# Position rows of the first expert table on ScalarE, and the adds of token pairs one pair later

## The chip, the cores and the metric

The kernel runs on one core of one Trainium2 chip. The metric is the device time of one launch in microseconds (us), lower is better; times of a kernel are given as the median of several runs. A profiled execution gives, beside its time, a trace of every instruction on the engines: TensorE (PE, with its weight loads as PEld), VectorE (DVE), ScalarE (ACT), GpSimd (POOL), and the DMA queues.

## What is computed

The reference is two transformer-like blocks over 256 tokens of width 1024, in float32. The change is in the last step of the second block, a retrieval of single-neuron experts:

```python
ts, ti = lax.top_k(s, K)                       # 16 best of 128 keys, twice per head, 8 heads
cs, ci = lax.top_k(cand.reshape(B, L, PEER_HEADS, K * K), K)
e1 = jnp.take_along_axis(ti[..., 0, :], ci // K, axis=-1)
e2 = jnp.take_along_axis(ti[..., 1, :], ci % K, axis=-1)
experts = e1 * N_KEYS + e2                     # 128 of 16384 experts per token
g = jax.nn.softmax(cs, axis=-1)
act = gelu(einsum('td,tkd->tk', xt, u_tab[experts])) * g
out = einsum('tk,tkd->td', act, v_tab[experts])
```

The kernel doesn't gather. It multiplies all tokens with the whole first table `u_tab` (16384 x 1024), takes the Gelu, multiplies by a dense table of weights that is zero for experts which a token didn't choose, and multiplies the result with the whole second table.

## The kernel before

**Units.** The weights come as blocks of 128x1024, 512 KB each, in one stream. `Stream.next` hands out a block as two parts whose sum is the float32 value: ScalarE casts the high part `wh` (line 244), VectorE subtracts it from the raw block to give the low part `wl` (line 251). It prepares them ahead: when unit n is asked for, the cast and the subtraction of unit n+3 are written into the queues of the two engines. There are three raw buffers, four of `wh`, four of `wl`. A unit of the first expert table is one product of 24 matmuls of 256 columns (`gemm_w`, lines 310 to 312). Two units fill one PSUM tile (`mm`, two buffers); behind the second one ScalarE takes the Gelu of both (line 1433) and its queue issues the store of the result to DRAM (line 1435).

**The dense weights.** The stage of the first expert table has 88 units; in the bursts behind the first 84 of them `weights_dense` builds `gd`, 128 x 128 x 256: first index by second index by token. For token t the rows of `eT` hold the 128 chosen first indices, second indices and weights. `o1` holds for each choice the row of zeros with a one at its first index (called position rows here), made for four tokens at once by a comparison with `iota` (line 1558; `ONE` is 4, two buffers). `oh` is the same for the second index, times the weight, in a high and a low half (line 1563; six buffers). Four steps later (`LAG`) a matmul of the two gives the token's 128x128 weights, halves side by side (line 1573). Two tokens share a PSUM tile (`acc`, three buffers). When the second of a pair is done, ScalarE copies the low halves into `gd` (line 1578) and VectorE adds the high halves (line 1579). The tile comes free when both have read it.

**Order.** Each engine works through its own queue in the order in which the program is written; a wait at the head of a queue holds all behind it. `paced` (line 1587) spreads the 260 steps of `weights_dense` (256 tokens and the lag) over 84 bursts, one behind each unit: three steps, in eight of the bursts four. So PE does 24 matmuls of a unit, three or four of L1573, then the next unit; ScalarE does the Gelu (behind every second unit), the copies of the burst, the cast for the next request; VectorE does the subtraction, then `o1`, `oh` and the add of each step.

Behind the stage comes the second expert table, which reads `gd`.

Of the kernel before, what the change touches and what calls it, by code (L numbers as in the profile page):

```python
# [10 lines left out]
F32 = mybir.dt.float32  # L11
# [4 lines left out]
AF = mybir.ActivationFunctionType  # L16
ALU = mybir.AluOpType
# [12 lines left out]
ONE = 4  # L30
# [237 lines left out]
class Pump:  # L268
# [3 lines left out]
    def add(self, gen, last=False):  # L272

        (self.last if last else self.active).append(gen)
# [15 lines left out]
def body(ctx, tc, a, o, upto=99):  # L290
    nc = tc.nc
# [6 lines left out]
    def psum(tag):  # L298
        return PS.tile([128, 512], F32, tag=tag, name=tag, bufs={"mm": 2, "acc": 3, "od": 1, "tr": 2}[tag])

    def accs():
        return [psum("acc"), psum("acc"), psum("acc"), psum("od")]
# [37 lines left out]
    def gemm_rows(acc, w, xh, xl, start, stop):  # L340
        h, lo = w
        for tt in range(2):
            ts_ = slice(tt * 128, tt * 128 + 128)
            for hf in range(2):
                cs = slice(hf * 512, hf * 512 + 512)
                mm3(acc[2 * tt + hf], xh[:, ts_], xl[:, ts_], h[:, cs], lo[:, cs], start, stop)

    def split(h, lo, src, eng=None):
        nc.scalar.copy(h, src)  # L349
        (eng or nc.vector).tensor_tensor(lo, src, h.bitcast(F32), op=ALU.subtract)  # L350
# [34 lines left out]
    def gain(i, pool):  # L385
        g = pool.tile([128, D], F32, tag="gain", name="gain", bufs=1)
        nc.gpsimd.dma_start(g, a["gains"][i:i + 1, :].to_broadcast([128, D]))
        return g
# [291 lines left out]
    with tc.tile_pool(name="mix", bufs=1) as MP:  # L680
# [285 lines left out]
        for c in range(8):  # L966
# [4 lines left out]
            t = sg[0][:, c, :]  # L971
# [25 lines left out]
        g = gain(POSTM, MP)  # L997
# [88 lines left out]
    with tc.tile_pool(name="b2", bufs=1) as BP:  # L1086
# [291 lines left out]
        for i in range(4):  # L1378
# [5 lines left out]
            t = th[:, 2 * i:2 * i + 2, :]  # L1384
# [37 lines left out]
    iota = PP.tile([128, 128], F32, name="iota")  # L1422
    eT = [PP.tile([128, 3, 128], F32, name=f"eT{tt}") for tt in range(2)]
    stored = [DP.tile([128, 8 if i < 15 else 4, T], F32, name=f"act{i}") for i in range(16)]

    def experts_in(i, between=pump.step):
        pt = psum("mm")
        gemm_w(pt[:, :T], ws.next(), xs_x)
        between()
        gemm_w(pt[:, T:], ws.next(), xs_x)  # L1430
        st = PP.tile([128, 2, T], F32, tag="st", name="st", bufs=2)
        last[i] = st
        nc.scalar.activation(st, pt.rearrange("p (e t) -> p e t", e=2), AF.Gelu_apprx_tanh)  # L1433
        if i < 62:
            nc.scalar.dma_start(stored[i // 4][:, 2 * (i % 4):2 * (i % 4) + 2, :], st)
# [3 lines left out]
    with tc.tile_pool(name="route", bufs=1) as RP:  # L1439
# [3 lines left out]
        v = RP.tile([128, 2, 16, 16], F32, name="v")  # L1443
# [99 lines left out]
    with tc.tile_pool(name="dense", bufs=1) as GP:  # L1543
        gd = GP.tile([128, 128, T], F32, name="gd")

        wp = GP.tile([128, 2, 128], F32R, name="wp")

        def weights_dense():

            o1s, ohs = {}, {}  # L1550
            for t in range(T + LAG):
                if t < T:
                    tt, tl = divmod(t, 128)
                    if tl == 0:
                        split(wp[:, 0], wp[:, 1], eT[tt][:, 2])
                    if t % ONE == 0:
                        o1 = GP.tile([128, ONE, 128], F32R, tag="oh1", name="oh1", bufs=2)
                        nc.vector.tensor_tensor(o1, iota[:, None, :].to_broadcast([128, ONE, 128]),  # L1558
                                                eT[tt][:, 0, tl:tl + ONE, None].to_broadcast([128, ONE, 128]),
                                                op=ALU.is_equal)  # L1560
                        o1s[t // ONE] = o1
                    oh = GP.tile([128, 2, 128], F32R, tag="ow", name="oh2", bufs=6)
                    nc.vector.scalar_tensor_tensor(oh, iota[:, None, :].to_broadcast([128, 2, 128]),  # L1563
                                                   eT[tt][:, 1, tl:tl + 1],
                                                   wp[:, :, tl:tl + 1].bitcast(F32).to_broadcast([128, 2, 128]),
                                                   op0=ALU.is_equal, op1=ALU.mult)
                    ohs[t] = oh
                u = t - LAG
                if u >= 0:
                    if u % 2 == 0:  # L1570
                        pt = psum("acc")
                    oh = ohs.pop(u)
                    nc.tensor.matmul(pt[:, u % 2 * T:u % 2 * T + T], o1s[u // ONE][:, u % ONE],  # L1573
                                     oh.rearrange("p n e -> p (n e)"), start=True, stop=True)
                    if u % 2 == 1:
                        v = pt.rearrange("p (t n e) -> p n e t", t=2, n=2)
                        g = gd[:, :, u - 1:u + 1]
                        nc.scalar.copy(g, v[:, 1])  # L1578
                        nc.vector.tensor_tensor(g, v[:, 0], g, op=ALU.add)  # L1579
                yield  # L1580

        pump.add(weights_dense())
        left = 128 - 2 * n_in[0]
        total = T + LAG
        busy = left - 4

        def paced(i):
            for _ in range(min(i + 1, busy) * total // busy - min(i, busy) * total // busy):
                pump.step()

        sv = {}

        def fetch(b):
            if b < 16:
                sv[b] = P0.tile([128, 8, T], F32, tag="lT" if b % 2 else "hT", name="sv")
                nc.gpsimd.dma_start(sv[b][:, :8 if b < 15 else 4, :], stored[b])

        order = list(range(124, 128)) + list(range(124))

        def act_split(n):  # L1600
            e = order[n]
            src = last[e // 2] if e >= 124 else sv[e // 8][:, e % 8 - e % 2:e % 8 - e % 2 + 2, :]
            if e % 2 == 0:
                nc.vector.tensor_tensor(src, src, gd[:, e:e + 2, :], op=ALU.mult)  # L1604
            ah = GP.tile([128, T], F32R, tag="ow", name="ah", bufs=6)
            al = GP.tile([128, T], F32R, tag="ow", name="al", bufs=6)
            split(ah, al, src[:, e % 2])
            if e % 8 == 7 and e < 120:
                fetch(e // 8 + 2)
            return ah, al  # L1610

        for i in range(left // 2):
            experts_in(n_in[0] + i, lambda: paced(2 * i))
            paced(2 * i + 1)
            if i == left // 2 - 2:
                pump.drain()
                ws.pool_every = 0
                nxt = [act_split(0), act_split(1)]
        fetch(0)
        fetch(1)  # L1620
        acc = accs()
        for n in range(126):
            nxt.append(act_split(n + 2))
            ah, al = nxt.pop(0)
            gemm_rows(acc, ws.next(), ah, al, n == 0, False)
        gf = P0.tile([128, D], F32, tag="raw", name="gf", bufs=RAW)
        nc.scalar.dma_start(gf, a["gains"][FINAL:FINAL + 1, :].to_broadcast([128, D]))
        x2 = [P0.tile([128, D], F32, tag="raw", name="x2", bufs=RAW) for tt in range(2)]
        for tt in range(2):
            nc.scalar.dma_start(x2[tt], res[tt * 128:(tt + 1) * 128, :])  # L1630
        finish(acc, [(ws.next(), *nxt[n]) for n in range(2)])
        jk = P0.tile([128, 1024], F32, tag="wh", name="jk", bufs=NH)
        ys = [P0.tile([128, D], F32, tag="wl", name="ys", bufs=NL) for tt in range(2)]
        rs = [None, None]

        def scaled(tt, hf):
            y = ys[tt][:, HALVES[hf]]
            if hf:
                nc.scalar.activation(y, y, AF.Copy, scale=rs[tt])
            else:  # L1640
                nc.vector.tensor_scalar(y, y, rs[tt], None, op0=ALU.mult)
            (nc.scalar if tt and hf else nc.sync).dma_start(o[tt * 128:tt * 128 + 128, HALVES[hf]], y)

        for tt in range(2):
            fn = RowNorm(GP, lambda hf: x2[tt][:, HALVES[hf]], jk[:, :512], 1.0)
            for hf, sl in enumerate(HALVES):
                nc.vector.tensor_tensor(x2[tt][:, sl], acc[2 * tt + hf], x2[tt][:, sl], op=ALU.add)
                fn.part(hf)
            if tt:
                scaled(0, 0)  # L1650
                scaled(0, 1)
            for sl in HALVES:
                nc.vector.tensor_tensor(ys[tt][:, sl], x2[tt][:, sl], gf[:, sl], op=ALU.mult)
            rs[tt] = fn.root()
        for hf in range(2):
            scaled(1, hf)
# [19 lines left out]
```

## Time and profile before

| | us |
|---|---|
| median of 3 runs | 1751.85 (1751.81 to 1753.88) |
| the profiled execution | 1750.99 |
| its span, first to last instruction | 1749.1 |
| busy PE / PEld | 1716.1 / 1571.1 |
| busy DVE / ACT / POOL | 1305.2 / 928.7 / 141.8 |
| the stage of the change, from 1104 to 1383 | 279 |

Busy time is the time in which at least one instruction of the engine was recorded. Matmuls are pipelined and their records overlap, so a PE that is busy all the time need not run at its peak; the distance between the starts of two matmuls tells that better. Records of the other engines overlap a little too, so what an instruction costs in a full queue is the distance from its start to the next one's.

### The profile page before, as it was taken

The page shows a single profiled execution, that of the slowest core. Times are in us where ns is not written, and L with a number is a line of the kernel's source. Part 1 is how long each engine was busy: PE and PEld are TensorE (multiplying, and loading weights), DVE is VectorE, ACT ScalarE, POOL GpSimd, SP SyncE. Part 2 cuts the span into 40 slices and gives each one's busy share as a digit, 9 for nine tenths or more (in the row PEclk, how much of TensorE's full clock was granted, in tenths as well). Part 3 has the DMA queues.
Part 4 walks back from the last instruction along what each step waited for, and adds up shares of the span by engine and source line. Part 5 has one row for each costly group of instructions (what it writes and reads, how often), then busy time and mean ns, then how long its engine had stood idle before and what let it go on. Part 6 is the DMA issues. An engine that isn't in the chain of part 4 may idle for free.

```text
span 1749.1 us, 30357 instructions
## 1 busy us (share of the span) xinstructions
PE 1716.1 (98%) x11768; PEld 1571.1 (90%) x11770; DVE 1305.2 (75%) x2238; ACT 928.7 (53%) x1518; POOL 141.8 (8%) x138
## 2 busy tenths in 40 slices
PE   8999999999999999999999999999999999999998
PEld 8999899999899987997899999999999988888886
DVE  5665677846765654878777999899999866667775
ACT  5544556654564445687345455555555545555444
POOL 2000000000100211000005624000000000000000
PEclk9999999999999999999899999999999999999999
DMA  7656454444476653563265576666665677777674
GB/s 246 189 172 198 149 181 147 141 148 138 137 227 190 195 166 119 169 194 109 74 193 196 184 226 216 221 193 199 194 199 188 215 250 250 238 252 240 241 243 166
DMA packets 93409, 332.05 MB, mean 190 GB/s; under 512 B 10553, under 2 KB 10708, under 8 KB 90961
## 3 DMA queue, kind: packets, MB, share of 16 engines
q1 hardware_dynamic: 79488, 287.73, 51.4%
q0 software_dynamic: 3696, 21.67, 3.5%
q10 hardware_dynamic: 10080, 20.71, 3.2%
q8 instruction: 92, 1.51, 0.4%
q14 instruction: 53, 0.43, 0.1%
HBM read 311.73 MB, written 18.35 MB: 189 GB/s over the span
## 4 chain that ended last, share of the span: by engine, by line
PE 78%; DVE 16%; issue 3%; ACT 1%; DMA 1%; POOL 0%; POOLq 0%; ACTq 0%; DVEq 0%
PE mm L310 13%; PE mm L312 13%; PE mm L311 13%; PE acc L312 8%; PE acc L310 8%; PE acc L311 8%; DVE oh L1563 5%; DVE wl L251 4%; PE od L310 2%; PE od L311 2%; PE od L312 2%; DVE gd L1579 2%; DVE oh L1558 2%; PE tr L1317 1%; PE acc L731 1%
## 5 line engine op out<-in xcount | busy, mean ns | idle before, releaser
L251 DVE TENSOR_TENSOR wl<-raw,wh 128x1024 fp32r<-128x1024 f32 x509 | 621.7, 1225 | 281.6 <-ACT wh L244 280.0
L310 PE MATMUL mm<-hT,wh 128*128 128x256 f32 (+1 forms) x2496 | 711.2, 285 | 0.4 <-ACT qb L1474 0.4
L311 PE MATMUL mm<-lT,wh 128*128 128x256 f32 (+1 forms) x2496 | 703.1, 282 | 0.0
L312 PE MATMUL mm<-hT,wl 128*128 128x256 f32 (+1 forms) x2496 | 702.7, 282 | 0.0
L244 ACT CAST wh<-raw 128x1024 fp32r<-128x1024 f32 x544 | 569.0, 1050 | 189.5 <-PE mm L311 71.4
L310 PEld LDWEIGHTS mm<-hT,wh 128*128 128x128 f32 x2496 | 471.7, 189 | 8.3 <-issue 3.9
L311 PEld LDWEIGHTS mm<-lT,wh 128*128 128x128 f32 x2496 | 470.5, 188 | 3.4 <-issue 1.4
L312 PEld LDWEIGHTS mm<-hT,wl 128*128 128x128 f32 x2496 | 472.1, 189 | 0.1
L310 PE MATMUL acc<-wh,ah 128*128 128x512 f32 x516 | 201.8, 391 | 0.0
L312 PE MATMUL acc<-wh,al 128*128 128x512 f32 x516 | 201.8, 391 | 0.0
L311 PE MATMUL acc<-wl,ah 128*128 128x512 f32 x516 | 201.6, 391 | 0.0
L349 ACT CAST ah<-sv 128x256 fp32r<-128x256 f32 x124 | 50.3, 406 | 152.6 <-DVE sv L1604 120.6
L312 PEld LDWEIGHTS acc<-wh,al 128*128 128x128 f32 x516 | 96.8, 188 | 20.8
L1563 DVE SCALAR_TENSOR_TENSOR oh<-iota,eT,wp 128x256 fp32r<-128x256 f32 x256 | 115.4, 479 | 0.0
L311 PEld LDWEIGHTS acc<-wl,ah 128*128 128x128 f32 x516 | 96.9, 188 | 19.6 <-issue 0.2
L310 PEld LDWEIGHTS acc<-wh,ah 128*128 128x128 f32 x516 | 97.0, 188 | 19.2 <-issue 0.3
L251 POOL TENSOR_TENSOR wl<-raw,wh 128x1024 fp32r<-128x1024 f32 x35 | 83.7, 2401 | 60.5 <-ACT wh L244 59.4
L1433 ACT ACTIVATE st<-mm 128x512 f32<-128x512 f32 x64 | 38.3, 599 | 94.3 <-PE mm L312 94.2
L350 DVE TENSOR_TENSOR al<-sv,ah 128x256 fp32r<-128x256 f32 x124 | 52.5, 424 | 35.0 <-ACT ah L349 35.0
L1578 ACT COPY gd<-acc 128x256 f32<-128x256 f32 x128 | 46.6, 402 | 59.3 <-PE acc L1573 43.4
L310 PE MATMUL od<-wh,ah 128*128 128x512 f32 x172 | 67.3, 391 | 0.0
L312 PE MATMUL od<-wh,al 128*128 128x512 f32 x172 | 67.2, 391 | 0.0
(400 smaller groups left out, 2041.9 us busy)
## 6 DMA issues: line engine op xcount, KB each, us to landing
raw<-in_ws_dram SPq DMA_DIRECT2D x288, 512.0 KB, 3.7
raw<-in_us_dram SPq DMA_DIRECT2D x128, 512.0 KB, 3.7
raw<-in_vs_dram SPq DMA_DIRECT2D x128, 512.0 KB, 4.2
act<-st ACTq DMA_DIRECT2D x62, 256.0 KB, 2.8
sv<-act POOLq DMA_DIRECT2D x15, 1024.0 KB, 7.1
gate_w<-in_gate_w_dram ACTq DMA_DIRECT2D x2, 1024.0 KB, 5.9
gain<-in_gains_dram POOLq DMA_DIRECT2D x3, 512.0 KB, 6.6
res<-x SPq DMA_DIRECT2D x2, 512.0 KB, 4.0
```

Of the source, the lines that this page charges most:

```text
L244: self.nc.scalar.copy(h, self.raw[i])
L251: eng.tensor_tensor(lo, self.raw.pop(i), h.bitcast(F32), op=ALU.subtract)
L310: nc.tensor.matmul(out, lh, rh, start=start, stop=False)
L311: nc.tensor.matmul(out, lh, rl, start=False, stop=False)
L312: nc.tensor.matmul(out, ll, rh, start=False, stop=stop)
L349: nc.scalar.copy(h, src)
L350: (eng or nc.vector).tensor_tensor(lo, src, h.bitcast(F32), op=ALU.subtract)
L1433: nc.scalar.activation(st, pt.rearrange("p (e t) -> p e t", e=2), AF.Gelu_apprx_tanh)
L1558: nc.vector.tensor_tensor(o1, iota[:, None, :].to_broadcast([128, ONE, 128]), eT[tt][:, 0, tl:tl + ONE, None].to_broadcast([128, ONE, 128] ...
L1563: nc.vector.scalar_tensor_tensor(oh, iota[:, None, :].to_broadcast([128, 2, 128]), eT[tt][:, 1, tl:tl + 1], wp[:, :, tl:tl + 1].bitcast(F3 ...
L1578: nc.scalar.copy(g, v[:, 1])
L1579: nc.vector.tensor_tensor(g, v[:, 0], g, op=ALU.add)
```

## The change

In `weights_dense` every second group of four tokens has its position rows made on ScalarE: four activations Abs(e - iota), one for each token, with the index as an operand per partition, and one Relu(1 - that) over all four, in place. The other groups stay on VectorE. The add of a token pair isn't written behind the copy of the same pair any more but behind the copy of the next pair; the last one comes after the loop.

```diff
-            o1s, ohs = {}, {}
+            o1s, ohs, copied = {}, {}, []
+
+            def add():
+                g, v = copied.pop(0)
+                nc.vector.tensor_tensor(g, v, g, op=ALU.add)
...
                         o1 = GP.tile([128, ONE, 128], F32R, tag="oh1", name="oh1", bufs=2)
-                        nc.vector.tensor_tensor(o1, iota[:, None, :].to_broadcast([128, ONE, 128]),
-                                                eT[tt][:, 0, tl:tl + ONE, None].to_broadcast([128, ONE, 128]),
-                                                op=ALU.is_equal)
+                        if t // ONE % 2:
+                            for j in range(ONE):
+                                nc.scalar.activation(o1[:, j], iota, AF.Abs, scale=-1.0,
+                                                     bias=eT[tt][:, 0, tl + j:tl + j + 1])
+                            nc.scalar.activation(o1, o1.bitcast(F32), AF.Relu, scale=-1.0, bias=1.0)
+                        else:
+                            nc.vector.tensor_tensor(o1, iota[:, None, :].to_broadcast([128, ONE, 128]),
+                                                    eT[tt][:, 0, tl:tl + ONE, None].to_broadcast([128, ONE, 128]),
+                                                    op=ALU.is_equal)
...
                         nc.scalar.copy(g, v[:, 1])
-                        nc.vector.tensor_tensor(g, v[:, 0], g, op=ALU.add)
-                yield
+                        copied.append((g, v[:, 0]))
+                        if len(copied) > 1:
+                            add()
+                yield
+            add()
```

## Rows read from the trace of the kernel before

**Rows 1.** Busy time by stage: length, then each engine's busy us and instructions.

```profile
core 0: us, PE busy (x) PEld busy (x) DVE busy (x) ACT busy (x) POOL busy (x), PEclk, DMA share, GB/s
1104.00:1383.00 279.00, 273.51 (x2254) 268.44 (x2254) 278.99 (x534) 148.56 (x255) 0.00 (x0) 1.00 0.62 198
```

**Rows 2.** Groups by line, VectorE, same stage: count, busy us, mean ns, idle before.

```profile
L1563 DVE SCALAR_TENSOR_TENSOR oh<-iota,eT,wp 128x256 fp32r<-128x256 f32 x256 | 115.4, 479 | 0.0
L251 DVE TENSOR_TENSOR wl<-raw,wh 128x1024 fp32r<-128x1024 f32 x84 | 102.2, 1217 | 0.8 <-ACT wh L244 0.8
L1579 DVE TENSOR_TENSOR gd<-acc,gd 128x256 f32<-128x256 f32 x128 | 55.8, 437 | 0.0
L1558 DVE TENSOR_TENSOR oh<-iota,eT 128x512 fp32r<-128x512 f32 x64 | 43.7, 683 | 0.0
```

**Rows 3.** Waits, same stage: who waited for whom, total us, times, longest.

```profile
PE acc L1573 <- DVE oh L1563: 3.6, 14, 0.5
...
DVE wl L251 <- ACT wh L244: 0.8, 1, 0.8
```

**Rows 4.** The matmuls of line 1573: duration in ns, first and last start.

```profile
L1573 PE MATMUL acc<-oh,oh x256: 279/282/385, 1105.8 to 1381.2; 128*128 128x256 f32 x128
```

**Rows 5.** Timeline of PE, line 1573 alone: start, length, engine, line, merged count.

```profile
1244.08 0.36 PE L1573 MATMUL acc<-oh,oh 128*128 128x256 f32 x1 [0.52 <-DVE oh L1563]
1247.08 0.52 PE L1573 MATMUL acc<-oh,oh 128*128 128x256 f32 x3
1250.29 0.52 PE L1573 MATMUL acc<-oh,oh 128*128 128x256 f32 x3
1253.49 0.52 PE L1573 MATMUL acc<-oh,oh 128*128 128x256 f32 x3
```

**Rows 6.** Timeline of VectorE in the middle of the stage.

```profile
1243.45 0.88 DVE L1563 SCALAR_TENSOR_TENSOR oh<-iota,eT,wp 128x256 fp32r<-128x256 f32 x2
...
1246.51 0.43 DVE L1579 TENSOR_TENSOR gd<-acc,gd 128x256 f32<-128x256 f32 x1
1246.86 0.68 DVE L1558 TENSOR_TENSOR oh<-iota,eT 128x512 fp32r<-128x512 f32 x1
1247.46 0.48 DVE L1563 SCALAR_TENSOR_TENSOR oh<-iota,eT,wp 128x256 fp32r<-128x256 f32 x1
1247.85 1.22 DVE L251 TENSOR_TENSOR wl<-raw,wh 128x1024 fp32r<-128x1024 f32 x1
1248.99 0.48 DVE L1563 SCALAR_TENSOR_TENSOR oh<-iota,eT,wp 128x256 fp32r<-128x256 f32 x1
```

**Rows 7.** Timeline of ScalarE over the same two bursts.

```profile
1247.28 0.60 ACT L1433 ACTIVATE st<-mm 128x512 f32<-128x512 f32 x1 [2.22 <-PE mm L312]
1247.91 0.33 ACTq L1435 DMA_DIRECT2D act<-st  x1
1248.28 0.69 ACT L1578 COPY gd<-acc 128x256 f32<-128x256 f32 x2 [0.40 <-ACT st L1433]
1248.83 1.06 ACT L244 CAST wh<-raw 128x1024 fp32r<-128x1024 f32 x1
1250.72 0.40 ACT L1578 COPY gd<-acc 128x256 f32<-128x256 f32 x1 [0.83 <-PE acc L1573]
1251.01 1.05 ACT L244 CAST wh<-raw 128x1024 fp32r<-128x1024 f32 x1
```

**Rows 8.** Timeline of ScalarE in earlier stages: activations with an operand per partition.

```profile
265.93 0.63 ACT L785 ACTIVATE ov<-tr,ls 128x128 f32<-128x128 f32 x2
...
762.04 0.52 ACT L1154 ACTIVATE aa<-rr,ncd 128x272 f32<-128x272 f32 x1
762.59 0.52 ACT L1155 ACTIVATE rr<-rr,cdec 128x272 f32<-128x272 f32 x1
763.02 0.41 ACT L1156 ACTIVATE ii<-aa 128x272 f32<-128x272 f32 x1
```

**Rows 9.** Table loads of the Gelu's line, and a square near the end.

```profile
L1433 ACT ACT_TABLE_LOAD  x2: 1283/1283/1283, 1022.3 to 1074.9; - x2
...
1739.24 0.64 ACT L424 ACTIVATE jk<-x 128x512 f32<-128x512 f32 x1 [6.02 <-DVE x L1647]
```

## The prediction

> **What bounds the kernel now.** I read the busy time by stage first. In the stage of the change, 1104 to 1383 us, VectorE (DVE) is busy 278.99 of 279.00 us, ScalarE (ACT) 148.56 and PE 273.51, at a granted clock of 1.00 (2.4 GHz) [rows 1]. So two engines look full, and the groups by line say with what: DVE makes 84 `wl`, 256 `oh`, 64 groups of position rows and 128 adds [rows 2]. The waits then tell DVE and PE apart: DVE waits once, for 0.8 us, while PE waits for DVE's `oh` 14 times [rows 3]. PE's own speed stands between undisturbed bursts: 1247.08, 1250.29 and 1253.49 are 54 matmuls in 6.41 us, 0.1187 us each [rows 5]. From the first L1573 matmul to the last, 1105.8 to 1381.2, lie 255 of them and 82 x 24 of the units, 2223 x 0.1187 = 263.9 of 275.4 us [rows 4]. So **PE loses about 11.5 us** here. That is the most that any relief of DVE can give in this stage.
>
> From start to start a DVE `wl` takes 1.14 us, an `oh` 0.39, a position group 0.60, an add 0.35 [rows 6]; 84 x 1.14 + 256 x 0.39 + 64 x 0.60 + 128 x 0.35 = 278.8. DVE is the bound, by its sum.
>
> **Part 1: every second position group goes to ScalarE.** Removed: 32 x 0.60 = 19.2 us of DVE, which leaves 259.6, less than PE's 263.9. Added: 32 times four Abs of 128x128 and one Relu of 128x512. No Abs or Relu is in the trace. The nearest row of the Abs' size, with an operand per partition as the Abs' bias is one, is L785: two in 0.63 us, so 0.26 from start to start and 0.37 whole [rows 8]. The Relu works in place on what the Abs wrote. L1155 overwrites what L1154 still reads and starts 0.55 after it, 0.03 behind its end; L1156, free of L1155, starts 0.43 after it, 0.09 before its end [rows 8]. So the fourth Abs counts 0.37 + 0.03 = 0.40, and the Relu, by a 128x512 ScalarE row of 0.64 [rows 9], counts 0.54, or 0.65 if its bias of 1.0 is an operand (the 0.11 between L1154 and L1156). The group is 3 x 0.26 + 0.40 + 0.54 to 0.65, I take **1.8 us**; from below four at 0.26 and a Relu at 0.54, 1.6; from above 4 x 0.40 + 0.72 = 2.3. All 32: 58 us, ScalarE 148.6 + 58 = 207 of 279. By its sum it isn't the bound. The Abs adds no wait: its buffer was last read by the matmul that the copy ahead of it in the queue has just waited for.
>
> What counts is what is queued behind. ScalarE works in order, and behind each burst stands the `wh` cast of the unit four ahead; DVE's `wl` waits for that cast, and all DVE work of the next burst stands behind that `wl`. Take E as the start of a burst's first matmul. Behind the second unit of a pair (E = 1247.08) the Gelu starts at E + 0.20, its store's issue holds the queue, the copies start at E + 1.20, the cast at E + 1.75, and it ends at E + 2.81; behind a first unit (E = 1250.29) the copy starts at E + 0.43 and the cast ends at E + 1.77 [rows 5, 7]. The position group goes in ahead of the cast in both.
>
> **Part 2: the add behind the next pair's copy.** No instruction is added but one call at the end. The add no longer waits for the copy just issued. Its price is elsewhere: the PSUM buffer of a pair (`acc`, three of them) comes free with its add. Before, the add stood five steps ahead of the matmul that takes the buffer again; now three. A burst is three steps (84 bursts, 260 steps: eight have four). So PE's burst j+2 needs adds that DVE makes in its section j+1, right behind the `wl` that waits for the cast of burst j.
>
> **The two together.** Let C be the cast's end, counted from E of burst j. PE starts burst j+2 at E + 6.40. It follows DVE by 0.15 (an `oh` from 1243.45, one of two in 0.88, ends 1243.93; its matmul starts 1244.08) [rows 5, 6]. DVE needs 0.03 and the `wl` (1.14), then its steps up to the add that PE wants, three steps ahead of a pair's first matmul, the last add whole (0.43). That matmul is the third of burst j+2 (at 6.64) if the burst begins with a pair, else the second (6.52). 1.20 is where ScalarE is free behind the Gelu, 0.28 a copy's share of two in 0.69, 1.05 the cast [rows 7]. t is the first step of a group on ScalarE:
> - t first in a gelu burst: C = 1.20 + 1.80 + 0.28 + 1.05 = 4.33. DVE then does `oh`, add, an even position group, `oh`, `oh`, add: 2.55. Ready at 4.33 + 1.17 + 2.55 = 8.05; PE wants it at 6.64 - 0.15 = 6.49. **1.56 late.**
> - t second: one copy more, C = 4.61; `oh`, `oh`, add, 1.21: 6.99 against 6.37, 0.62 late.
> - t third: C = 4.33; `oh`, add, `oh`, `oh`, add, 1.95: 7.45 against 6.49, 0.96 late.
> - in the other bursts, t first (its Abs start behind the cast of the burst before): C = 2.63, in time; second: C = 3.72, in time; third: C = 3.56, 0.19 late.
>
> A group comes each eight steps, bursts are three, their kinds alternate and the four-step ones shift the phase, so all six places are equally frequent: 3.33 us for six, 32 / 6 x 3.33 = **17.8 us**. Eight four-step sections are 1.14 + 4 x 0.39 + 2 x 0.35 + 0.30 = 3.70 of DVE against PE's 28 x 0.1187 = 3.32; with no slack left there, 8 x 0.38 = 3.0 more. Sum 20.8 us of stalls where there are 11.5: **+9.3 us**. Nothing behind the stage changes; it starts that much later. The profiled execution (span 1749.1, 1750.99 with what lies around it) would become 1760.3; on the median of 1751.85, **1761.2**. With the group at 1.6 the late terms are 1.36, 0.42, 0.76 and 0: 13.5 + 3.0 - 11.5 = +5; if the four-step sections find slack too, +2. At 2.3 they are 2.06, 1.12, 1.46 and 0.69, and the two places in time become late by 0.36 and 0.23: 31.6 + 3.0 - 11.5 = +23. Own range: 1754 to 1775.
>
> The Trainium skill (Perfetto Trace Analysis, section Optimizing Scalar/DVE Operations) says that with DVE saturated, giving some of its work to ScalarE may make sense; on busy sums alone that speaks for a gain, and it is the first rival. Its section Optimization Strategy says that a gap which keeps coming back on the engine that should be full can mean too few PSUM buffers; by the steps above that would be the sight of the changed stage.
>
> **Rivals.**
> 1. *Faster: PE becomes the bound.* If DVE's relief counts and the casts come in time, PE runs at 0.1187 per matmul and the 11.5 us go: 1740. For it: 207 of 279 us on ScalarE, and DVE 4 us below PE. Against it: DVE would have to wait almost nowhere, since its slack is 0.05 us per burst, and C = 4.3 to 4.6 in half of the places. Two of those three come in time only if a group costs ScalarE under about 0.8 us. Half the loss given back would be 1746.
> 2. *No difference.* The late casts meet a DVE that is still behind from before, so that part of the lateness isn't waited for; stalls then change owner, from `oh` to adds, at about the old 11.5 us: 1750 to 1755.
> 3. *The change doesn't do what it says: table loads.* If Abs or Relu were outside of the Gelu's table, each group would cost two loads of 1.28 us [rows 9], 32 x 2.57 = 82 us on ScalarE: 289 us and its 40 pauses of 0.4 behind the Gelu's store issue, 305 us for a stage of 279: 1778 at least. Against it: the squares at 1739 run with no load since the one for the Gelu at 1074.9 [rows 9]. The Trainium skill (ScalarE: Activation LUTs, section Table sets) states that relu and abs are in every set; no row of before has either.
>
> **How the numbers follow.** Forecast 0.70, rival 1 0.14, rival 2 0.13, rival 3 0.03. What a measurement of this kernel tells from no change is about 0.2%, 3.5 us. Faster by more than that is rival 1, 0.14; within it most of rival 2 and the forecast's low edge, 0.15; slower 0.71. The range takes the forecast's own and reaches down into rival 2; rival 1, rival 3 and the last of the high end are left out: 1750 to 1772.
>
> **What would show it.** Right: in the new stage DVE idles 20 us or more, nearly all in front of L251 on the `wh` cast; PE's waits at L1573 grow to some 21 us and name the add rather than `oh`, in stalls of 0.6 to 1.6 us a burst or two behind a ScalarE group in a gelu burst; the ScalarE group takes 1.7 to 1.9 us; the stage is 286 to 291 us long. Wrong: a stage of 268 us with DVE idle in many short waits (rival 1); or PE's waits unchanged (rival 2); or ACT_TABLE_LOAD in the stage (rival 3). The weakest step is that DVE stands waiting when a late cast comes: if it is still busy with earlier work at C, the lateness counts less.

## The result and the profile after

The changed kernel takes 1768.43 us (median of 4 runs, 1764.48 to 1770.54), the kernel before 1751.83 beside it: ratio 1.010, 95% interval 1.0085 to 1.0116. It is slower by 16.6 us, inside the range of 1750 to 1772; the forecast was 9.3 us of loss. The span of the profiled execution went from 1749.1 to 1766.2. No median or ratio here or below has in it three single executions of e1, e2 and e8 that took 3436 to 7906 us.

The stage by busy time (length, then each engine's busy us and instructions, granted clock, DMA), then the matmuls of line 1573 before, now line 1586 (duration in ns, first and last start), then what PE's two sequences, the weight loads and the matmuls, waited for in front of them:

```profile
1104.00:1400.00 296.00, 277.70 (x2258) 271.55 (x2257) 262.55 (x501) 203.15 (x415) 0.00 (x0) 0.99 0.60 186
```

```profile
L1586 PE MATMUL acc<-oh,oh x256: 277/282/387, 1106.1 to 1398.3; 128*128 128x256 f32 x128
```

```profile
  DVE gd L1556: 29.3, 43
  ACT wh L244: 5.9, 3
```

The same list for line 1573 before:

```profile
  issue: 6.7, 19
  DVE oh L1563: 3.6, 14
  ACT gd L1578: 1.6, 3
  ACT st L1433: 1.5, 3
  ACT wh L244: 0.7, 1
```

The new stage is 17 us longer than the old one in [rows 1], and first to last matmul of the token pairs take 292.2 us where they took 275.4 [rows 4]: the whole loss is here, +16.8. At 0.1187 us per matmul 263.9 of it is PE's own, so PE loses 28.3 us where it lost 11.5. VectorE (DVE), which was busy for 278.99 of 279.00 us [rows 1], is idle for 33.4 of 296. And PE now waits for the add, `gd` of line 1556; before, no wait for the add is in the list. These lists add up both sequences of PE, and most stalls stand in both, once for the weight load and once for the matmul, sometimes under two names: the 5.9 us for the cast are three weight loads whose matmuls wait for the add. So 29.3 isn't a time lost; 28.3 is, and it has everything in it.

The groups of the stage by line (count, busy us, mean ns, idle before and for whom):

```profile
L251 DVE TENSOR_TENSOR wl<-raw,wh 128x1024 fp32r<-128x1024 f32 x84 | 102.3, 1217 | 31.4 <-ACT wh L244 31.4
L1567 ACT ACTIVATE oh<-iota,eT 128x128 fp32r<-128x128 f32 x128 | 40.9, 395 | 2.4 <-ACT st L1433 2.4
L1569 ACT ACTIVATE oh<-oh 128x512 fp32r<-128x512 f32 x32 | 20.3, 633 | 1.0
```

DVE's idle time stands in front of the subtraction, 31.4 us where it was 0.8 [rows 2]: it waits for ScalarE's cast. One place shows the chain. ScalarE, then VectorE, then the matmuls of line 1586, in three views of the same stretch (start, length, engine, line, merged count, idle before):

```profile
1354.21 0.40 ACT L1591 COPY gd<-acc 128x256 f32<-128x256 f32 x1 [0.40 <-ACT st L1433]
1354.50 1.27 ACT L1567 ACTIVATE oh<-iota,eT 128x128 fp32r<-128x128 f32 x4
1355.80 0.63 ACT L1569 ACTIVATE oh<-oh 128x512 fp32r<-128x512 f32 x1
1356.34 0.36 ACT L1591 COPY gd<-acc 128x256 f32<-128x256 f32 x1
1356.59 1.05 ACT L244 CAST wh<-raw 128x1024 fp32r<-128x1024 f32 x1
```

```profile
1357.67 1.23 DVE L251 TENSOR_TENSOR wl<-raw,wh 128x1024 fp32r<-128x1024 f32 x1 [1.48 <-ACT wh L244]
1358.81 0.88 DVE L1576 SCALAR_TENSOR_TENSOR oh<-iota,eT,wp 128x256 fp32r<-128x256 f32 x2
1359.60 0.42 DVE L1556 TENSOR_TENSOR gd<-acc,gd 128x256 f32<-128x256 f32 x1
1359.94 0.68 DVE L1571 TENSOR_TENSOR oh<-iota,eT 128x512 fp32r<-128x512 f32 x1
1360.54 0.48 DVE L1576 SCALAR_TENSOR_TENSOR oh<-iota,eT,wp 128x256 fp32r<-128x256 f32 x1
1360.93 1.22 DVE L251 TENSOR_TENSOR wl<-raw,wh 128x1024 fp32r<-128x1024 f32 x1
1362.07 0.48 DVE L1576 SCALAR_TENSOR_TENSOR oh<-iota,eT,wp 128x256 fp32r<-128x256 f32 x1
1362.46 0.42 DVE L1556 TENSOR_TENSOR gd<-acc,gd 128x256 f32<-128x256 f32 x1
```

```profile
1353.02 0.52 PE L1586 MATMUL acc<-oh,oh 128*128 128x256 f32 x3
1356.22 0.65 PE L1586 MATMUL acc<-oh,oh 128*128 128x256 f32 x3
1359.51 0.28 PE L1586 MATMUL acc<-oh,oh 128*128 128x256 f32 x1
1360.17 0.47 PE L1586 MATMUL acc<-oh,oh 128*128 128x256 f32 x2 [0.38 <-DVE gd L1556]
1363.03 0.35 PE L1586 MATMUL acc<-oh,oh 128*128 128x256 f32 x1 [2.39 <-DVE gd L1556]
1367.58 0.52 PE L1586 MATMUL acc<-oh,oh 128*128 128x256 f32 x3
```

The burst at E = 1353.02 is one behind a second unit with the ScalarE group at its second step. The group holds the queue from 1354.50 to 1356.34, 1.84 us. The cast, which would have followed the copy, ends 1357.64, E + 4.62. DVE stood for 1.48 us, then needs the subtraction, two `oh` and the add, done at 1360.02, and the second matmul of the burst at 1359.51 starts at 1360.17, about 0.54 late. The fourth matmul of that burst is the one that the prediction had not costed: it wants the add of 1362.46, made in this same burst's section, behind the next subtraction, and starts 2.86 us after the second.

### The profile page after: what moved, and what is told of

It is laid out like the page before. It is cut to its first block, busy times and chain, and to the rows that moved or that the text cites. A ratio compares the mean times of both kernels' runs of the same rounds, so it can differ in the third digit from the quotient of the medians.

```text
span 1766.2 us, 30545 instructions
## 1 busy us (share of the span) xinstructions
PE 1720.2 (97%) x11770; PEld 1573.7 (89%) x11770; DVE 1287.7 (73%) x2206; ACT 982.7 (56%) x1678; POOL 142.1 (8%) x138
## 4 chain that ended last, share of the span: by engine, by line
PE 87%; DVE 5%; ACT 4%; issue 3%; DMA 1%; POOL 0%; ACTq 0%; POOLq 0%; DVEq 0%
PE mm L310 16%; PE mm L312 16%; PE mm L311 16%; PE acc L312 8%; PE acc L310 7%; PE acc L311 7%; PE od L310 2%; PE od L311 2%; PE od L312 2%; PE acc L1586 1%; DVE oh L1576 1%; ACT wh L244 1%; ACT oh L1567 1%; PE tr L1317 1%; PE acc L731 1%
## 5 line engine op out<-in xcount | busy, mean ns | idle before, releaser
L312 PEld LDWEIGHTS acc<-wh,al 128*128 128x128 f32 x516 | 96.9, 188 | 20.8
L311 PEld LDWEIGHTS acc<-wl,ah 128*128 128x128 f32 x516 | 96.9, 188 | 19.8 <-issue 0.2
L1586 PE MATMUL acc<-oh,oh 128*128 128x256 f32 x256 | 52.0, 294 | 18.3 <-DVE gd L1556 18.3
```

The lines of the kernel that those rows point to most:

```text
L311: nc.tensor.matmul(out, lh, rl, start=False, stop=False)
L312: nc.tensor.matmul(out, ll, rh, start=False, stop=stop)
```

## The experiments

Theory A is the prediction's: the cast comes late behind the ScalarE group, DVE stands behind the cast, and the later add leaves PE too little room to absorb that. Theory B: ScalarE's longer queue alone makes the loss. Theory C: the later add alone makes it. All ratios are to the kernel before, on the same chip, with 95% intervals. "PE loses" is first to last matmul of the token pairs in the profile, less 0.1187 us for each matmul between (2223 with 84 bursts, 2271 with 87).

| kernel | median us | ratio | PE loses, us |
|---|---|---|---|
| before | 1751.8 (1751.2 to 1752.1 beside the others) | 1 | 11.5 |
| the change | 1768.4 | 1.0085 to 1.0116 | 28.3 |
| e1 rows alone | 1750.6 | 0.9982 to 1.0006 | 10.7 (e12) |
| e2 adds alone | 1754.2 | 0.9999 to 1.0032 | 13.4 |
| e3 four tiles | 1749.9 | 0.9974 to 1.0005 | 10.2 |
| e4 cast first | 1756.3 | 1.0016 to 1.0046 | 15.7 |
| e5 no four-step bursts | 1762.5 | 1.0052 to 1.0096 | 19.3 |
| e6 before, no four-step bursts | 1749.8 | 0.9985 to 1.0011 | 8.3 |
| e7 every third, in time | 1743.2 | 0.9942 to 0.9974 | 1.6 |
| e8 every third, late | 1763.3 | 1.0044 to 1.0092 | 21.6 |
| e9 as e7, later add | 1753.4 | 0.9993 to 1.0015 | 11.2 |
| e10 four-step bursts even | 1759.0 | 1.0020 to 1.0048 | 18.4 |
| e11 four-step bursts odd | 1769.8 | 1.0088 to 1.0122 | not read so |

In e3 a quarter of the matmuls writes another tag, and the first and the last are taken over both; in e11 the last one stands behind the stage.

### Each part alone: e1 and e2

e1 takes the later add back out of the change:

```diff
                         copied.append((g, v[:, 0]))
-                        if len(copied) > 1:
-                            add()
+                        add()
```

> Part 1 alone: every second position group on ScalarE, the add at once behind its own pair's copy, as before the change. Theory A (late cast behind the ScalarE group, met by adds that stand only three steps ahead of the tile's next use): with five steps of room the lateness is absorbed, PE loses about 9 us in the stage where it loses 11.5 before, so 1746 to 1752, DVE idle some 20 us in the stage. Theory B (ScalarE's longer queue alone makes the loss, whatever the adds do): about 1766 to 1770, as with the whole change. Theory C (the later add alone makes it, ScalarE's group is harmless): PE's bound, 1740 to 1746.

e2 leaves all position groups on VectorE and keeps the later add:

```diff
-                        if t // ONE % 2:
-                            for j in range(ONE):
-                                nc.scalar.activation(o1[:, j], iota, AF.Abs, scale=-1.0,
...
-                        else:
```

> Part 2 alone: all position groups on VectorE, the add of a pair behind the copy of the next pair. Theory A: DVE stays the bound (278.8 us of work) and the casts are in time; the shorter room for the tile costs a little at the longest sections, 1 to 3 us, so 1752 to 1756. Theory B: no change, 1750 to 1753. Theory C: nearly the whole loss, 1763 to 1770.

Measured: 1750.6 and 1754.2. Neither part alone makes the loss: e1 can't be told from before, e2 is some 2.5 us above it at the edge of what can be told, and the two together cost 16.6. B and C fall; it is the meeting of the two. The later add isn't free by itself, though. In e2 too PE's matmuls (line 1580 there) wait for it:

```profile
PE acc L1580 <- DVE gd L1556: 6.7, 7, 1.7
```

Four bursts of e2, all with four steps and all beginning in the middle of a pair, lose 1.92, 1.81, 1.78 and 1.84 us; before, the same four lose 2.6 together. PE loses less in the other bursts, so the sum hardly moves.

e12 is the kernel of e1 once more, for its profile:

> The kernel of e1 once more, for its profile: PE's waits in the stage about 9 us, no stall over 1 us, DVE idle about 20 us, and 1746 to 1752 by theory A.

It took 1749.99. Its matmuls of the pairs and the waits in front of them:

```profile
L1586 PE MATMUL acc<-oh,oh x256: 279/281/388, 1105.8 to 1380.4; 128*128 128x256 f32 x128
```

```profile
  ACT st L1433: 4.9, 6
  DVE oh L1576: 4.4, 8
```

With ScalarE's same work PE loses 10.7 us, not 28.3, and among its waits is none for an add. DVE stands for 7.4 us on late casts and for 7.7 on late copies, 15 us of the 279 in all, where I expected 20; PE's longest single wait is 1.2 us (a weight load's), where I expected none over 1.

### The room of the add: e3

A fourth tile gives the add its five steps back:

```diff
                     if u % 2 == 0:
-                        pt = psum("acc")
+                        pt = psum("od" if u // 2 % 4 == 3 else "acc")
```

> The whole change with a fourth PSUM tile for the token pairs (the idle tile of tag od takes every fourth pair), so that an add stands five steps ahead of its tile's next use again. Theory A: PE's waits for the adds (29 us with the change) go nearly to zero, some 8 us of waits for oh come in their place, 1746 to 1752. Theory B: no difference to the change, 1766 to 1770. Theory C: as with theory A or less, down to 1740.

Measured 1749.9, with this among the waits of PE in the stage:

```profile
PE acc L1586 <- DVE oh L1576: 5.3, 9, 1.0
```

The waits for the adds (29.3 us in both sequences) are gone, and with them 18 us; DVE still waits for late casts, 18.4 us in 23 places. So the tile is what turns a late cast into a stall of PE, as the Trainium skill's rule in the prediction has it (Perfetto Trace Analysis, section Optimization Strategy: gaps that come back can mean too few PSUM buffers). It isn't a gain over before all the same: with the tiles out of the way, PE waits for `oh` behind the same late casts.

### The cast ahead of the group: e4

```diff
-            experts_in(n_in[0] + i, lambda: paced(2 * i))
+            experts_in(n_in[0] + i, lambda: (ws.early(), paced(2 * i)))
+            ws.early()
             paced(2 * i + 1)
```

(`early` writes only the cast of the next unit; its subtraction follows with the next request.)

> The whole change with three tiles, and the cast of the unit four ahead written into ScalarE's queue ahead of the burst's copies and position group instead of behind them (its subtraction stays where it is). Theory A: the late term goes, what stays are the four-step bursts and the copies that now stand behind a cast: 1750 to 1757, DVE's waits on the cast from 31 us to under 10. Theory B (ScalarE has the same work): 1764 to 1770. Theory C: no difference to the change, 1766 to 1770.

Measured 1756.3. DVE's waits on the cast fell from 31.4 to 4.0 us and most of the loss is gone with them, but what was behind the cast now comes late itself, as PE's waits show:

```profile
PEld acc L1594 <- ACT oh L1577: 11.2, 12, 1.1
PE acc L1594 <- ACT oh L1577: 8.8, 12, 0.9
```

PE waits some 11 us in 12 places for the ScalarE group's Relu (line 1577 here; the two rows are the same places, seen by the weight loads and by the matmuls), where the change has no matmul that waits for its Relu. The order in ScalarE's queue decides which of the two is late, not that one is.

### The four-step bursts: e5, e6, e10, e11

```diff
-        busy = left - 4
+        busy = left - 1
```

> The whole change, with its 260 steps spread over 87 bursts in place of 84, so that no burst has four steps (all have three, the first two). In a four-step burst that starts in the second half of a pair, the fourth matmul wants a tile whose add was written in the same burst, behind the subtraction that waits for the cast of the burst before; with the change the longest stalls, up to 2.4 us, stand there. If these bursts, and not the late casts in three-step bursts, make what I had undersized, some 12 to 16 us come back against the change and its clock stays whole: 1751 to 1758. If only the late casts in general count: 1763 to 1769.

> The kernel before with the same spread over 87 bursts: control for the spread. DVE does the same work over three units more, so it loses less per unit: 3 to 6 us faster than before, 1746 to 1749. If the spread does nothing for a DVE-bound stage: 1751 to 1753.

Measured 1762.5 (e5) and 1749.8 (e6). Some 6 us of the change's loss come back (9.0 by what PE loses in the two profiled executions), between my two numbers, and the spread itself does nothing that can be told for the kernel before. In e5 the bursts repeat with a period of eight, and their stalls are these two in each (line 1586 again):

```profile
1180.62 0.40 PE L1586 MATMUL acc<-oh,oh 128*128 128x256 f32 x2
1181.23 0.39 PE L1586 MATMUL acc<-oh,oh 128*128 128x256 f32 x1 [0.21 <-DVE gd L1556]
1184.25 0.52 PE L1586 MATMUL acc<-oh,oh 128*128 128x256 f32 x3
1187.46 0.40 PE L1586 MATMUL acc<-oh,oh 128*128 128x256 f32 x2
1188.75 0.38 PE L1586 MATMUL acc<-oh,oh 128*128 128x256 f32 x1 [0.89 <-DVE gd L1556]
```

An undisturbed burst lasts 3.20; these last 3.63 and 4.35, so 1.58 us are lost in eight bursts.

e10 and e11 keep the 84 bursts and move the four-step ones to where the burst begins with a pair (even), or in the middle of one (odd):

```diff
+        sizes = []
+        for i in range(busy):
+            done = sum(sizes)
+            sizes.append(4 if (i + 1) * total // busy - done > 3 and done % 2 == 0 else 3)
```

(e11 has `== 1`.)

> The whole change, 84 bursts, eight of four steps, but the four-step bursts put only where the burst begins with a pair (an even step), so that its fourth matmul is the second of a pair and wants no tile. If the four-step bursts that begin in the middle of a pair make the longest stalls: no stall over 2 us, no drop of the clock, 6 to 9 us faster than the change, 1759 to 1763. If every four-step burst counts alike, or none: 1766 to 1770.

> The opposite of e10: four-step bursts only where the burst begins in the middle of a pair (seven of them, the last step is made at the end of the stage). If the start decides: stalls of 2 us and more behind most of them, and the clock falls after those; 1770 to 1777. If not: 1766 to 1770.

Measured 1759.0 (e10), 9.4 us under the change, at the lower edge of what I expected, and 1769.8 (e11), which can't be told from the change and is just under what I expected. In e10 the longest wait of PE is 1.4 us, and the clock stays at 1.00 in the whole stage. The matmuls of its pairs:

```profile
L1586 PE MATMUL acc<-oh,oh x256: 277/282/387, 1106.1 to 1388.4; 128*128 128x256 f32 x128
```

A four-step burst that begins in the middle of a pair asks, with its fourth matmul, for a tile whose add stands in its own section; one that begins with a pair doesn't. The change has four of the first kind, and their own excess over 3.32 us is 1.81, 1.28, 4.04 and 4.75, 11.9 together. The seven of e11 lose 19.8, but the change has four more that begin with a pair, and these lose 4.6 with the bursts right behind them, so the two kernels come out alike. In e10 the eight that begin with a pair, with those behind them, lose 7.3.

### The place of the group: e7, e8, e9

These have 87 bursts and every third group on ScalarE; twelve steps are four bursts, so the group keeps its place. e7 and e8 make the adds at once and differ in one digit:

```diff
-                        if t // ONE % 2:
+                        if t // ONE % 3 == 0:
```

(e8 has `== 2`.)

> No later add (adds as before), 87 bursts, and every third position group on ScalarE. Twelve steps are four bursts, so the place of the ScalarE group in its burst is nearly fixed; here it is the middle step of the burst behind a first unit, one of the places that my steps call in time. DVE is left with about 266 us of work in the old stage's terms, PE with 264. If the place decides (theory A): PE runs nearly without stalls, 10 to 12 us faster than before, 1739 to 1743. If only the engines' sums or ScalarE's load decide: the same time as its twin e8.

> The twin of e7: the same instructions, but the groups with the other remainder, which puts the ScalarE group at the first step of the burst behind a second unit, behind the Gelu, the latest place by my steps (1.56 us). Theory A: DVE waits on the cast behind each group, PE loses some 15 us against e7, 1753 to 1758. If only sums decide: as e7.

Measured 1743.2 and 1763.3: 20 us apart with the same instructions but for one group more or less. The matmuls of e7's pairs and what PE's sequences waited for, then the same of e8 with the matmuls' wait alone:

```profile
L1586 PE MATMUL acc<-oh,oh x256: 279/281/384, 1106.6 to 1377.8; 128*128 128x256 f32 x128
```

```profile
  ACT gd L1591: 1.9, 1
  DVE oh L1576: 1.7, 1
```

```profile
L1586 PE MATMUL acc<-oh,oh x256: 277/282/414, 1106.0 to 1397.2; 128*128 128x256 f32 x128
```

```profile
  DVE oh L1576: 16.4, 21
```

e7 runs without a stall up to the end of the stage, where the last three steps are made at once and cost its 1.6 us. It beats the kernel before by 0.42% (0.26 to 0.58%), and so the changed one too. In e8 PE loses about one us behind every group, where its matmuls wait for `oh`. It lost 5 us more than I expected, by another way too: DVE hardly waits for the cast there (1.2 us) but in its adds, 18.5 us for ScalarE's copy, which also stands behind the group:

```profile
L1556 DVE TENSOR_TENSOR gd<-acc,gd 128x256 f32<-128x256 f32 x128 | 57.4, 449 | 18.5 <-ACT gd L1591 18.5
```

e9 is e7 with the change's later add:

> As e7 (every third group on ScalarE, at the place in time, 87 bursts), but with the add behind the next pair's copy. Theory A: three steps of room instead of five are too few at this place too when the longer sections come; PE loses about 7 us against e7, 1748 to 1752. If the later add costs nothing where the group is in time: as e7, 1741 to 1745.

Measured 1753.4, ten us above e7 and a little above my range: in nearly every fourth burst one stall that costs 0.4 to 0.5 us, on the add. One of them, DVE and then PE; the burst with the ScalarE group starts at E = 1168.19:

```profile
1171.98 1.22 DVE L251 TENSOR_TENSOR wl<-raw,wh 128x1024 fp32r<-128x1024 f32 x1 [0.59 <-ACT wh L244]
1177.93 0.41 DVE L1556 TENSOR_TENSOR gd<-acc,gd 128x256 f32<-128x256 f32 x1
1178.39 0.39 PE L1586 MATMUL acc<-oh,oh 128*128 128x256 f32 x1 [0.20 <-DVE gd L1556]
```

The cast ends at E + 3.75, as the steps have it (3.72), but DVE stands 0.59 us for it, and three bursts on its add is late. So the place that the steps call in time is in time for five steps of room (e7) and not for three.

## Why the prediction was right, and what was mis-sized

- *What bounds the stage.* Right. DVE was the bound before; with 19 us of its work gone it isn't, and PE's loss moved from `oh` to the add.
- *The ScalarE group, 1.8 us.* It measures 1.84 from its first Abs to the next instruction's start. The last table load of the Gelu's line is at 1075.2, ahead of the stage, so rival 3 didn't occur. The Trainium skill (ScalarE: Activation LUTs, section What ACT_TABLE_LOAD costs) gives an activation with an operand per partition about 280 ns and 0.833 per element, by estimate 387 for the Abs; the trace has 395, and agrees.
- *When the cast ends.* Right to some hundredths: the place shown above was forecast at E + 4.61 and is 4.62; in e5 a group at the first step, E = 1180.62, was forecast at 4.33, and DVE starts behind its cast at 1185.00, E + 4.38.
- *That DVE stands waiting when a late cast comes*, named as the weakest step: it does, 31.4 us in 30 places.
- *The late casts in three-step bursts, 17.8 us.* Too much: the bursts of the change that neither have four steps nor come next after one lose 12.3 us. I had added up the six places as if each met an undisturbed PE. They come two or three bursts apart, and a stall from one moves the burst that the next is measured against: in e5 three of the places come in turn, and 1.58 us are lost per eight bursts where the steps give 2.52. The first-step place loses 1.15 for 1.56, since its own burst had lost 0.43; the third-step place (0.96) loses nothing, since its own burst is the one held up for 1.15. And the 0.43 is from a place that the steps call in time, the second step of a burst behind a first unit: they look at the burst two on, and the late add is for the third one on, as in e9.
- *The four-step bursts, 3.0 us.* This is the step that failed. I costed only their longer section for DVE. With a tile wanted by the fourth matmul of the same burst, the chain through cast, subtraction and add has one burst less of room. This is the later add's own price: e2, with no group on ScalarE, has it too, 7.4 us in four bursts. The seven four-step bursts between first and last matmul lose 12.7 us over their 3.32 and those right behind them 3.8 more: 16.5. That is a count by place, and late casts of the groups fall into these bursts as well; what the start in the middle of a pair makes of it is what e10 shows, 9.4 us, with the clock's 3.2 (below) among them.
- *The clock*, for which the sum had no term: after the two longest stalls of the change PE ran at half speed for about 3.4 us each. The rest of those two bursts, once the stalls are taken off, is 3.2 us over its usual length, and is part of the 16.5.
- So 20.8 us of stalls were forecast and 28.3 (12.3 + 16.5, within the rounding of the starts) came; +9.3 was +16.8, and the stage, forecast at 286 to 291 us, is 296 long.
- *Rival 1*, PE as the bound, is what e7 reaches (1.6 us lost); its condition, that casts and adds come in time, isn't met by the change. *Rival 2*, stalls that only change owner, has its time in e3 and e1, where PE loses 10.2 us and 10.7 (e12) for 11.5 before; but there the adds are in time and PE still waits for `oh`.

## What to carry to other kernels

Work that is moved to an engine with time to spare is paid for by what stands behind it in that engine's queue: find the next instruction there that somebody waits for (here a cast, 1.8 us later), and give it or its consumer room. A read that is put off keeps its buffer for as long; count in program steps how far ahead of the buffer's next use it stands, in the worst burst, not in the mean one, and for more than the next burst. Where work comes in a rhythm, a group that always falls into the slack place (every third here, not every second) can be worth more than more of it moved.

## What the hardware showed that was not expected

The granted clock by stretch around the stall of 2.39 us at 1360 to 1363 (length, busy times, then clock):

```profile
1362.00:1363.00 1.00, 0.00 (x0) 0.00 (x1) 1.00 (x4) 0.97 (x3) 0.00 (x0) 1.00 0.38 143
1363.00:1364.00 1.00, 0.97 (x6) 1.00 (x7) 1.00 (x4) 1.00 (x2) 0.00 (x0) 0.71 0.86 127
1364.00:1365.00 1.00, 1.00 (x7) 1.00 (x7) 1.00 (x3) 0.13 (x1) 0.00 (x0) 0.50 0.91 356
1365.00:1366.00 1.00, 1.00 (x6) 1.00 (x6) 1.00 (x3) 0.00 (x0) 0.00 (x0) 0.50 0.16 57
1366.00:1367.00 1.00, 1.00 (x8) 1.00 (x7) 0.68 (x2) 0.00 (x0) 0.00 (x0) 0.59 0.37 82
```

In this fall and in the other one of the change, the clock (1.00 is 2.4 GHz, 0.50 is 1.2) is still full while PE stands and halves only after PE has work again; what it lacks in the four rows adds up to about 3.4 us at half speed, in which the matmuls start 0.21 us apart in place of 0.12. In e6 it halves 0.1 us before PE has work again, so that order isn't a rule. It fell after both stalls of over two us in the change (2.31 and 2.39) and after two of the four in e11 (2.57 and 2.38, not after 2.39 and 2.33). After the waits of 1.63 us in the middle of the stage, in the change and in e11, it didn't; behind the last wait of the stage it fell after 1.57 us (e8), 1.63 (e6) and 2.45 (e9), and not after 1.72 (e7) and 2.46 (e5). What decides between two stalls of the same length no run here shows. Where it falls, a stall costs more than its own length: the two bursts of the change lose 4.04 and 4.75 us, their longest stalls 2.31 and 2.39.

The mean clock of a whole execution doesn't tell these falls. The profiled execution of the kernel before has a longer one far ahead of the stage, behind a pause of 2.7 us between two matmuls; that of e11 has the same pause there, and no fall. In this order:

```profile
853.00:861.00 8.00, 8.00 (x25) 6.74 (x24) 4.07 (x11) 1.02 (x3) 0.00 (x0) 0.50 0.11 41
850.00:860.00 10.00, 10.00 (x65) 9.38 (x66) 7.43 (x17) 2.64 (x6) 0.00 (x0) 1.00 0.16 54
```

Some 10 us at half speed cost about 5. So much lies between the executions of the kernel before with a mean clock of 0.999 (1745.6 to 1748.1 us) and those with 0.994 to 0.996 (1750.3 to 1754.2). Of the changed kernel's four executions the one with the highest mean clock (0.997, the others 0.994) is the fastest, 1764.48; the missing fall can be this one as well as one in the stage, and no run here shows which.
